# An HGRN2 and Fourier two-layer kernel: V made for four heads at a time with 512 streaming columns, heads' outputs and residual gates in DRAM

## The chip, the core and the metric

The kernel runs on one core of a Trainium2 chip. The metric is the device time of one execution in microseconds, the median over runs. A core has five engines that each work through their own queue of instructions in order: TensorE (PE in the profile, with its weight loads as PEld), VectorE (DVE), ScalarE (ACT), GpSimd (POOL) and SyncE (SP), which here issues all DMAs. [...] On-chip data lies in SBUF (128 partitions), results of TensorE in PSUM.

## The reference

Two layers on a latent sequence of 512 tokens with a width of 1024; a context of 256 tokens feeds the first. Each layer is normalized and modulated by adaLN vectors (from a conditioning vector by a matrix product), and its result is added through a residual gate, also from adaLN.

```
q = silu(p[0]);  f = lb + (1 - lb) * sigmoid(p[1:3]);  v = p[3];  z = p[4]     # p = h @ w_in, five streams
S = f * S + (1 - f) outer v;  o = q . S        # both directions, 16 heads of 128, context then latents
y = rms_norm(o) * silu(z);  x = x + gate * (y @ w_out)                          # layer 1 (HGRN2)
y = real(fft2(u)) * silu(z);  x = x + gate * (y @ w_out)                        # layer 2 (Fourier mixer)
out = rms_norm(x)
```

So for each head there are six products: q, two forget gates for the latents, the same two gates for the context, and z; and V, which is a plain product of tokens and a weight for all 768 tokens, with no nonlinearity and no head of its own until it is used.

## The kernel before

**Products.** Every f32 product is made as three matmuls on rounded parts (`mm3`, L94 to L97): high by high, high by low, low by high. A weight tile of 512 KB comes in as f32 (`wr`, a ring of three, loaded by SP at L70) and is split into `wh` on ScalarE (L56) and `wl` on VectorE (L57), each in a ring of three. `W.get` splits one tile ahead and loads three ahead, in the order of the list `specs`. The normalized tokens are held transposed and split (`hlh`, `hll` for the 512 latents, `hc` for the 256 context tokens).

**Start stage.** Up to about 60 us PE, ACT and DVE run an order that is written out by hand (`manual_schedule`): adaLN rows (`ada_load`, `ada_mm`), norms, transposes (`tp`, L232), modulation of the tokens (L238, L243, L245), and the first head's products (`first`) as the pieces come in. The pool `p0` holds what only this stage needs and is closed at its end, the pools of the heads (`sp`) are opened after it.

**Heads.** The generator `projections()` makes the weights' products of head after head in chunks; at each of its yields `advance()` emits one step of the scan of the head before it. So on PE chunks of products (the cover) alternate with short scan steps, which need ScalarE and VectorE between them. Per head the scan has, in this order: sums inside blocks of 32 (`cs`), six levels in which a matmul `gp` (L578) is followed by z = z * tt on VectorE (L586) and the rounding copy kk on ScalarE (L545), the states (`ktp`, `sp`), the output `op` (L638 to L640), its squares (ScalarE, L644), the power on POOL (L180), the scaled copy `os` (L648), four transposes `otp` (L652), and y = otp * norm gain * zs on VectorE (L656). Outside the hand-written start, the engines' orders are set by a scheduler, by its own estimates of costs.

**V.** `proj_v(pr)` runs once per pair of heads, between the products of the even and the odd head: two weight tiles [128, 4, 256], the six blocks of 128 tokens by 8 parts of the width by 3 matmuls, 144 matmuls of 256 streaming columns with the tokens as stationary operand; two blocks share one PSUM bank of 512 columns, and ScalarE copies each bank out (L440, 128x512, 24 times).

**y, gates, output.** Heads' outputs y (L656) stay in SBUF as pairs of 512 KB. The output product takes y in halves (`y_parts`, split at L56 and L57): round 0 for the first 256 tokens as filler during the last head's scan (`out0_early`, heads 0 to 12), round 1 after it (`out0_late`). Residual gates and the layer-2 modulation come from `ada_rest`, side work spread over the heads (32 loads `ar`, accumulated on VectorE into `acc`); a gate is acc, summed over partitions by a matmul with ones (`gtp`), kept as [128, 1024] in SBUF.

Of the kernel before, what the change touches and what calls it, by code (L numbers as in the profile page):

```python
# [7 lines left out]
F32 = mybir.dt.float32  # L8
# [24 lines left out]
def hgrn_fourier_kernel(ctx: ExitStack, tc: tile.TileContext, a):  # L33
# [25 lines left out]
    class Weights:  # L59
# [13 lines left out]
        def halves(self, n):  # L73
            while len(self.parts) <= min(n, len(self.specs) - 1):
                j = len(self.parts)
                self.loaded(j)
                shape, fold = self.specs[j][1:]
                if j == 3:
                    hi, lo = (py.tile(shape, F32R, tag=f"yp{6 + b}", name=f"wz{b}") for b in range(2))
                else:  # L80
                    hi = pw.tile(shape, F32R, tag="wh", name=f"wh{j}")
                    lo = pw.tile(shape, F32R, tag="wl", name=f"wl{j}")
                src = self.raw[j]
                if fold is not None:
# [26 lines left out]
    def ada_load(d):  # L111
        wa[d] = []
        for j in range(2):
            h = KT // 2
            if d < 4:
                w = py.tile([P, h, 256], F32, tag=f"yp{2 * d + j}", name=f"wa{d}_{j}")
            else:
                w = p0.tile([P, h, 256], F32, name=f"wa{d}_{j}")
# [127 lines left out]


    specs = []
    at = {}

    def spec(key, src, shape, fold=None):
        at[key] = len(specs)
        specs.append((src, shape, fold))

    for pr in range(NH // 2):
        for st in (1, 2, 0, 3):
            spec(("w", 2 * pr, st), a["hg_w"][2 * pr, st], [P, KT, P])
        for b in range(2):
            spec(("v", pr, b), a["hg_v"][pr, b], [P, 4, 256])
        for st in (1, 2, 0, 3):  # L260
            spec(("w", 2 * pr + 1, st), a["hg_w"][2 * pr + 1, st], [P, KT, P])
    for k in range(16):
# [103 lines left out]

    st_start.close()

    gates = [pc.tile([P, D], F32, tag=f"gate{j}", name=f"gate{j}") for j in range(2)]
    a1 = pc.tile([P, KT], F32, name="a1")  # L370
    b1 = pc.tile([P, KT], F32, name="b1")

# [4 lines left out]
    def ada_rest():  # L377
# [11 lines left out]
        for j in (0, 1, 2, 3):  # L389
# [14 lines left out]
            if j in (0, 3):  # L404
                for h in range(2):
                    q = psM(f"gtp{j}_{h}")
                    pe.matmul(q, ones[:, :P], acc[:, h * 512:(h + 1) * 512], start=True, stop=True)
                    s.activation(gates[0 if j == 0 else 1][:, h * 512:(h + 1) * 512], q, AF.Copy)
            else:
                q = psM(f"gtp{j}")  # L410
                for d in range(KT):
                    pe.matmul(q[:, d:d + 1], acc[:, d * P:(d + 1) * P], ones[:, 0:1], start=True, stop=True)
                if j == 1:
                    v.tensor_tensor(out=b1, in0=q[:, :KT], in1=vcol[:, 32:40], op=ALU.add)
                else:
# [5 lines left out]
    ypair = [None]  # L421
    rr = sp.tile([P, 2, TC], F32, name="rr")
    v.memset(rr, 1.0)

    def proj_v(pr):
        vt = sp.tile([P, NT + NTC, 256], F32, tag="vt", name=f"vt{pr}", bufs=2)
        vt_of[pr] = vt
        hl = [W.get(at["v", pr, b]) for b in range(2)]
        for m in range(0, NT + NTC, 2):
            ps_ = psP(f"vps{pr}_{m}")  # L430
            for i in range(2):
                n = m + i
                (th, tl), n0 = (hlat, n) if n < NT else (hctx, n - NT)
                for k in range(KT):
                    wh, wl = hl[k // 4]
                    lh, ll = th[k][:, n0 * P:(n0 + 1) * P], tl[k][:, n0 * P:(n0 + 1) * P]
                    mm3(ps_[:, i * 256:(i + 1) * 256], lh, ll, wh[:, k % 4, :], wl[:, k % 4, :], k == 0, k == KT - 1)
                if i == 0:
                    yield None
            s.activation(vt[:, m:m + 2, :].rearrange("p a b -> p (a b)"), ps_, AF.Copy)  # L440
            yield None

    def lat_proj(ps_, wh, wl, th, tl):
        for k in range(KT):
            mm3(ps_, wh[:, k, :], wl[:, k, :], th[:, k, :], tl[:, k, :], k == 0, k == KT - 1)
            if k == KT // 2 - 1:
                yield None

    def proj(i):
# [46 lines left out]
        for st, dst in ((0, q), (3, zs)):  # L496
            wh, wl = W.get(at["w", i, st])
            pl = psP(f"pq{i}_{st}")
            yield from lat_proj(pl, wh, wl, hlh, hll)
            silu(pl, dst)  # L500
            if st == 0:
                yield None
            else:
                yield scan(i, fl, z4, fc, q, zs)

    def scan(i, fl, z4, fc, q, zs):
# [143 lines left out]
        tp = psM(f"otp{i}")  # L650
        for n in range(NT):
            pe.transpose(tp[:, n * P:(n + 1) * P], os_[:, n, :], ident)  # L652
        if i % 2 == 0:
            ypair[0] = py.tile([P, 2, T], F32, tag=f"yp{i // 2}", name=f"y{i}")
        y = ypair[0][:, i % 2, :]
        v.scalar_tensor_tensor(out=y, in0=tp, scalar=ngc, in1=zs, op0=ALU.mult, op1=ALU.mult)  # L656
# [198 lines left out]
    for d in range(KT):  # L855
        for e in range(2):
# [106 lines left out]
def _layouts(x, c, ctx, c_ctx, ada_w, ada_b, norm_g, hg_w_in, hg_lb_logits, hg_norm_g, hg_w_out, ft_w_in,  # L963
# [67 lines left out]
```

## Time and profile before

| | |
|---|---|
| median of three runs (1207.1 to 1210.05) | 1209.47 us |
| profiled execution, its own time | 1208.84 us |
| span of its trace | 1207.0 us |
| mean granted TensorE clock | 0.995 |
| TensorE busy | 1186.8 us in 7677 matmul records |
| VectorE, ScalarE, GpSimd busy | 763.6, 562.6, 42.8 us |
| moved by DMA | 118.52 MB, mean 98 GB/s |

A matmul record's duration goes from its start to its modelled end, and several overlap. A row of the timeline has start, duration, engine, line, operation, output and inputs, size and count; the bracket at its end says how long the engine sat idle before it and what released it. In the groups the columns behind the bar are busy us, mean ns of one, and idle time before, with what ended most of it. f32 matmuls of the scan are recorded twice each, so that `x8` in the timeline is four of them in the program.

### The profile page before, as it was taken

How to read it: one execution, taken by the hardware profiler on the slowest of the kernel's cores; microseconds unless marked ns; L12 is line 12 of the kernel's file. 1: busy time of each engine (PE TensorE's matmuls, PEld its weight loads, DVE VectorE, ACT ScalarE, POOL GpSimd, SP SyncE). 2: the span in 40 equal slices, each digit the busy share in tenths (PEclk: the TensorE clock that was granted, in tenths of full speed). 3: DMA queues.
4: the chain of work that ended last, by engine and by line, in shares of the span. 5: the costliest groups of instructions: out<-in, count | busy, mean ns of one | idle time of the engine just before them, and what ended most of it. 6: DMA issues, size and time to landing. Idle time of an engine off the chain costs nothing.

```text
span 1207.0 us, 18983 instructions
## 1 busy us (share of the span) xinstructions
PE 1186.8 (98%) x7677; PEld 1050.8 (87%) x7677; DVE 763.6 (63%) x1250; ACT 562.6 (47%) x1130; POOL 42.8 (4%) x76
## 2 busy tenths in 40 slices
PE   8999999999999999999999999999999999999997
PEld 5699899899889989989988988998888998988885
DVE  5596654665765675686457547458576856668554
ACT  4455544554454453445445455355556533333322
POOL 2100000000000000000000000000000000000000
PEclk9999999999999999999999999999999999999999
DMA  9434211122511521242121112113555314333221
GB/s 358 183 123 141 71 53 53 53 71 70 168 59 31 174 78 53 71 140 71 36 70 53 35 54 70 37 53 107 163 179 182 111 43 134 108 108 120 88 87 70
DMA packets 33673, 118.52 MB, mean 98 GB/s; under 512 B 3879, under 2 KB 4144, under 8 KB 33586
## 3 DMA queue, kind: packets, MB, share of 16 engines
q1 hardware_dynamic: 33586, 117.32, 29.6%
q8 instruction: 60, 0.98, 0.3%
q14 instruction: 27, 0.22, 0.1%
HBM read 115.20 MB, written 2.10 MB: 97 GB/s over the span
## 4 chain that ended last, share of the span: by engine, by line
PE 90%; DVE 4%; DMA 2%; ACT 2%; issue 1%; POOL 1%; SPq 0%; DVEq 0%; POOLq 0%; ACTq 0%
PE gp L578 7%; PE pf L95 4%; PE pq L95 4%; PE pq L97 4%; PE pq L96 4%; PE pf L97 4%; PE pf L96 4%; PE vps L95 4%; PE vps L96 4%; PE vps L97 4%; PE pfc L95 2%; PE pfc L96 2%; PE pfc L97 2%; PE o0a L97 2%; PE o0a L95 2%; PE o0a L96 2%
## 5 line engine op out<-in xcount | busy, mean ns | idle before, releaser
L56 ACT ACTIVATE wh<-wr 128x1024 fp32r<-128x1024 f32 x140 | 148.0, 1058 | 229.9 <-PE pq L96 89.3
L57 DVE TENSOR_TENSOR wl<-wr,wh 128x1024 fp32r<-128x1024 f32 x140 | 170.7, 1220 | 100.4 <-ACT wh L56 100.2
L586 DVE TENSOR_TENSOR z<-z,tt 128x512 f32<-128x512 f32 x192 | 124.0, 687 | 122.3 <-PE gp L578 110.9
L578 PE MATMUL gp<-z,kk 128*128 128x128 f32 x768 | 103.5, 277 | 0.7 <-ACT kk L545 0.6
L578 PEld LDWEIGHTS gp<-z,kk 128*128 128x128 f32 x768 | 97.6, 191 | 6.7 <-ACT kk L545 3.3
L95 PE MATMUL pf<-hlh,wh 128*128 128x512 f32 x240 | 99.2, 413 | 0.0
L95 PE MATMUL pq<-hlh,wh 128*128 128x512 f32 x240 | 97.1, 405 | 0.0
L545 ACT ACTIVATE kk<-z 128x512 f32<-128x512 f32 x96 | 61.8, 644 | 71.5 <-DVE z L586 71.3
L97 PE MATMUL pf<-hlh,wl 128*128 128x512 f32 x240 | 94.5, 394 | 0.0
L97 PE MATMUL pq<-hlh,wl 128*128 128x512 f32 x240 | 93.9, 391 | 0.0
L96 PE MATMUL pf<-hll,wh 128*128 128x512 f32 x240 | 93.7, 391 | 0.0
L96 PE MATMUL pq<-hll,wh 128*128 128x512 f32 x240 | 93.5, 390 | 0.0
L95 PE MATMUL pfc<-hc,wh 128*128 128x256 f32 x256 | 74.8, 292 | 0.0
L95 PE MATMUL vps<-wh,hlh 128*128 128x256 f32 x256 | 74.2, 291 | 0.0
L97 PE MATMUL vps<-wh,hll 128*128 128x256 f32 x256 | 72.6, 283 | 0.0
L96 PE MATMUL vps<-wl,hlh 128*128 128x256 f32 x256 | 72.5, 283 | 0.0
L96 PE MATMUL pfc<-hc,wh 128*128 128x256 f32 x256 | 72.4, 283 | 0.0
L97 PE MATMUL pfc<-hc,wl 128*128 128x256 f32 x256 | 72.4, 283 | 0.0
L97 PEld LDWEIGHTS pf<-hlh,wl 128*128 128x128 f32 x240 | 45.0, 188 | 10.4 <-issue 0.2
L97 PEld LDWEIGHTS pq<-hlh,wl 128*128 128x128 f32 x240 | 45.1, 188 | 10.0
L95 PEld LDWEIGHTS pf<-hlh,wh 128*128 128x128 f32 x240 | 45.2, 188 | 9.5 <-issue 1.9
L96 PEld LDWEIGHTS pf<-hll,wh 128*128 128x128 f32 x240 | 45.3, 189 | 8.2 <-issue 0.2
(268 smaller groups left out, 2994.0 us busy)
## 6 DMA issues: line engine op xcount, KB each, us to landing
wr<-hg_w SPq DMA_DIRECT2D x64, 512.0 KB, 3.5
ar<-ada_r SPq DMA_DIRECT2D x32, 512.0 KB, 3.8
wr<-ft_w SPq DMA_DIRECT2D x32, 512.0 KB, 4.0
wr<-hg_wout SPq DMA_DIRECT2D x29, 512.0 KB, 3.5
wa<-ada_a SPq DMA_DIRECT2D x16, 512.0 KB, 10.5
wr<-hg_v SPq DMA_DIRECT2D x16, 512.0 KB, 3.4
wr<-ft_wout SPq DMA_DIRECT2D x16, 512.0 KB, 3.5
xs<-x SPq DMA_DIRECT2D x4, 512.0 KB, 3.7
```

What stands on the lines that cost most here:

```text
L56: s.activation(hi, src, AF.Copy)
L57: v.tensor_tensor(out=lo, in0=src, in1=hi.bitcast(F32), op=ALU.subtract)
L95: pe.matmul(out, lh, rh, start=first, stop=False)
L96: pe.matmul(out, lh, rl, start=False, stop=False)
L97: pe.matmul(out, ll, rh, start=False, stop=last)
L545: s.activation(view(kk, 0, [[2 * h, T // (2 * h)], [h, 2], [1, h]]), view(z4, 2 * T, [[2 * h, T // (2 * h)], [T + h, 2], [1, h]]), AF.Copy)
L578: pe.matmul(gp[:, n * P:(n + 1) * P], kk[:, n * P:(n + 1) * P], view(z4, n * P, dims), start=True, stop=True)
L586: v.tensor_tensor(out=za, in0=za, in1=ta, op=ALU.mult)
```

## The change

- **V.** `proj_v(qd)` runs for four heads at a time (before heads 1, 5, 9 and 13, in the place where pair 2 qd had it); the second pair of four has none. Four weight tiles [128, 2, 512] instead of twice two tiles [128, 4, 256]: the same bytes in the same number of tiles. 144 matmuls of 512 columns per four heads, token blocks in the order 4, 5, 0, 1, 2, 3 (the context first), one PSUM bank per block, copied out as two halves of 256 columns (48 times), each into the `vt` of a pair. The split parts of V's tiles have a ring of four of their own in the pool `sp`, and the second tile of V is split while head 0, 4, 8, 12 finishes its last product.
- **Chunks.** Products of q and z of heads 3, 7, 11 and 15 (`i % 4 == 3`) are cut after parts 1, 3 and 5 instead of once after 3.
- **y.** y of heads 0 to 12 goes to DRAM (`yd`, 256 KB each, a DMA on SP's queue) from one SBUF tile, and comes back in halves of [128, 256] for each of the two output rounds (`y_fetch`, two tiles, one fetch ahead).
- **Gates.** One row of each gate goes to DRAM (`grow`), and both are loaded back broadcast to 128 partitions after the loads of x.
- **adaLN tiles.** The sixteen half tiles `wa` use one ring of twelve in the start's pool; `wz` moves there, `ht` and `fg` to the last stages' pool.

```diff
-                    hi, lo = (py.tile(shape, F32R, tag=f"yp{6 + b}", name=f"wz{b}") for b in range(2))
+                    hi, lo = (p0.tile(shape, F32R, name=f"wz{b}") for b in range(2))
                 else:
-                    hi = pw.tile(shape, F32R, tag="wh", name=f"wh{j}")
-                    lo = pw.tile(shape, F32R, tag="wl", name=f"wl{j}")
+                    pool, depth = (sp, 4) if j in vsplit else (pw, 3)
+                    hi = pool.tile(shape, F32R, tag="wh", name=f"wh{j}", bufs=depth)
+                    lo = pool.tile(shape, F32R, tag="wl", name=f"wl{j}", bufs=depth)
...
+            w = p0.tile([P, h, 256], F32, tag="wa", name=f"wa{d}_{j}", bufs=12)
...
-        for b in range(2):
-            spec(("v", pr, b), a["hg_v"][pr, b], [P, 4, 256])
+        for b in range(4 if pr % 2 == 0 else 0):
+            vsplit.add(len(specs))
+            spec(("v", pr // 2, b), a["hg_v"][pr // 2, b], [P, 2, 512])
...
-                    s.activation(gates[0 if j == 0 else 1][:, h * 512:(h + 1) * 512], q, AF.Copy)
+                    s.activation(acc[0:1, h * 512:(h + 1) * 512], q[0:1, :], AF.Copy)
+                nc.sync.dma_start(out=grow[0 if j == 0 else 1], in_=acc[0:1, :])
...
+    def proj_v(qd):
+        vts = [sp.tile([P, NT + NTC, 256], F32, tag="vt", name=f"vt{qd}_{b}", bufs=3) for b in range(2)]
+        vt_of[2 * qd], vt_of[2 * qd + 1] = vts
+        hl = [W.get(at["v", qd, b]) for b in range(4)]
+        for n in (4, 5, 0, 1, 2, 3):
+            ps_ = psP(f"vps{qd}_{n}")
+            (th, tl), n0 = (hlat, n) if n < NT else (hctx, n - NT)
+            c = slice(n0 * P, (n0 + 1) * P)
+            for k in range(KT):
+                wh, wl = hl[k // 2]
+                mm3(ps_, th[k][:, c], tl[k][:, c], wh[:, k % 2, :], wl[:, k % 2, :], k == 0, k == KT - 1)
+            for b in range(2):
+                s.activation(vts[b][:, n, :], ps_[:, b * 256:(b + 1) * 256], AF.Copy)
             yield None
...
-            if k == KT // 2 - 1:
+            if k in stops:
                 yield None
...
-            yield from lat_proj(pl, wh, wl, hlh, hll)
+            yield from lat_proj(pl, wh, wl, hlh, hll, (1, 3, 5) if i % 4 == 3 else (3,))
+            if st == 3 and i % 4 == 0:
+                W.halves(at["v", i // 4, 1])
...
+        y = py.tile([P, T], F32, tag="y" if i < LAST else f"y{i}", name=f"y{i}")
         v.scalar_tensor_tensor(out=y, in0=tp, scalar=ngc, in1=zs, op0=ALU.mult, op1=ALU.mult)
+        if i < LAST:
+            nc.sync.dma_start(out=yd[i], in_=y)
...
+    def y_fetch(k, r, ahead):
+        for kk in range(min(LAST, k + 1 + ahead)):
+            if (kk, r) not in got:
+                t = got[kk, r] = (fp if r else sp).tile([P, 256], F32, tag="yr", name=f"yr{r}_{kk}", bufs=2)
+                nc.sync.dma_start(out=t, in_=yd[kk][:, r * 256:(r + 1) * 256])
+        return got[k, r]
...
     def projections():
         for pr in range(NH // 2):
             yield from proj(2 * pr)
-            yield from proj_v(pr)
+            if pr % 2 == 0:
+                yield from proj_v(pr // 2)
             yield from proj(2 * pr + 1)
...
+    for j in range(2):
+        gates[j] = fp.tile([P, D], F32, tag=f"gate{j}", name=f"gate{j}")
+        nc.sync.dma_start(out=gates[j], in_=grow[j].broadcast_to([P, D]))
```

Line numbers after are 1 to 16 higher (`mm3` L97 to L99, the splits L57 and L58, `gp` L581, `op` L641 to L643, `otp` L655).

**TensorE at the end of the start.** pfc_2 is the second context gate of head 0, vps_n a block of V, wh_714 and wh_729 the first V tile's high part, cs the block sums. Before:

```order
L95 MATMUL pfc_2_685<-hc_132,wh_288 128x256
L96 MATMUL pfc_2_685<-hc_134,wh_288 128x256
L97 MATMUL pfc_2_685<-hc_132,wl_289 128x256
L95 MATMUL vps_0_735<-wh_714,hlh 128x256
L96 MATMUL vps_0_735<-wl_715,hlh 128x256
L97 MATMUL vps_0_735<-wh_714,hll 128x256
```

After:

```order
L97 MATMUL pfc_2_700<-hc_134,wh_290 128x256
L98 MATMUL pfc_2_700<-hc_136,wh_290 128x256
L99 MATMUL pfc_2_700<-hc_134,wl_291 128x256
L97 MATMUL vps_4_763<-wh_729,hc_133 128x512
L97 MATMUL vps_5_820<-wh_729,hc_133 128x512
L97 MATMUL vps_0_863<-wh_729,hlh 128x512
L556 MATMUL cs_802<-ks_793,ones 32x128 x4
L97 MATMUL vps_1_902<-wh_729,hlh 128x512
L98 MATMUL vps_4_763<-wl_730,hc_133 128x512
L99 MATMUL vps_4_763<-wh_729,hc_135 128x512
```

Before, 28 matmuls on the first V half, split during the start, follow pfc_2. Now the next row after pfc_2 takes the first V tile, of which four products with the high part and the block sums stand ahead of the first with its low part.

**ScalarE at the same place.** fc is the context gate, zs the z gate of head 0, wh the V tiles' high parts, kk the first scan copy. Before:

```order
L455 ACTIVATE fc_644<-pfc_2_685 128x256
L456 ACTIVATE fc_644<-fc_644,lbc,omlb 128x256 x2
L472 ACTIVATE zs_646<-first_549 128x512
L56 ACTIVATE wh_723<-wr_718 128x1024
L56 ACTIVATE wh_729<-wr_720 128x1024
L545 ACTIVATE kk_2_770<-z_0_643 128x512
```

After:

```order
L456 ACTIVATE fc_659<-pfc_2_700 128x256
L457 ACTIVATE fc_659<-fc_659,lbc,omlb 128x256 x2
L473 ACTIVATE zs_661<-first_551 128x512
L57 ACTIVATE wh_729<-wr_698 128x1024
L57 ACTIVATE wh_739<-wr_733 128x1024
L57 ACTIVATE wh_745<-wr_735 128x1024
L57 ACTIVATE wh_751<-wr_743 128x1024
L548 ACTIVATE kk_2_800<-z_0_658 128x512
```

Four V splits stand in a row behind zs where two did, and the first of them is now the first V tile's (before, the second's; the first's stood in the start stage).

**TensorE between op and otp in head 2.** pq_3 is head 3's z product (before: pq_0 its q product), pfc_2 head 3's context gate, pf_1 head 4's first gate. Before, with left-out rows of the same kinds between:

```order
L638 MATMUL op_2052<-vt_1622,am_1697 128x128
L639 MATMUL op_2052<-st_1695,z_2_1260 128x128
L640 MATMUL op_2052<-st_1695,z_2_1260 128x128
L95 MATMUL pfc_2_2074<-hc_131,wh_1895 128x256
L96 MATMUL pfc_2_2074<-hc_133,wh_1895 128x256
L97 MATMUL pfc_2_2074<-hc_131,wl_1896 128x256
...
L95 MATMUL pq_0_2114<-hlh,wh_2004 128x512
L96 MATMUL pq_0_2114<-hll,wh_2004 128x512
L97 MATMUL pq_0_2114<-hlh,wl_2005 128x512
...
L652 MATMUL otp_2127<-ident,os_2065 128x128 x4
```

After:

```order
L641 MATMUL op_2006<-vt_1_738,am_1716 128x128
L642 MATMUL op_2006<-st_1714,z_2_1301 128x128
L643 MATMUL op_2006<-st_1714,z_2_1301 128x128
L99 MATMUL pq_3_1999<-hlh,wl_1898 128x512
L97 MATMUL pf_1_2074<-hlh,wh_1993 128x512
L98 MATMUL pf_1_2074<-hll,wh_1993 128x512
L99 MATMUL pf_1_2074<-hlh,wl_1994 128x512
...
L98 MATMUL pf_1_2074<-hll,wh_1993 128x512
L655 MATMUL otp_2047<-ident,os_2019 128x128
L99 MATMUL pf_1_2074<-hlh,wl_1994 128x512
L655 MATMUL otp_2047<-ident,os_2019 128x128 x2
```

Before, the whole of pfc_2 (24 matmuls of 256 columns) and twelve of pq_0 lie between; now one of pq_3 and eight of pf_1. Heads 6, 10 and 14 read alike (three and six in head 6).

More of the change, by code (lines that the diff above doesn't have):

```diff
@@ L40, in hgrn_fourier_kernel @@
     py = ctx.enter_context(tc.tile_pool(name="py", bufs=1))
+    pd = ctx.enter_context(tc.tile_pool(name="pd", bufs=1, space=bass.MemoryType.DRAM))
     pp = ctx.enter_context(tc.tile_pool(name="pp", bufs=1, space=PSUM))
@@ L114, in ada_load @@
             h = KT // 2
[L115 to L118, printed above, removed]
+            w = p0.tile([P, h, 256], F32, tag="wa", name=f"wa{d}_{j}", bufs=12)
             nc.sync.dma_start(out=w, in_=a["ada_a"][d][:, j * h:(j + 1) * h, :])
@@ L248, in hgrn_fourier_kernel @@
     specs = []
+    vsplit = set()
     at = {}
@@ L367, in hgrn_fourier_kernel @@
     st_start.close()
-    gates = [pc.tile([P, D], F32, tag=f"gate{j}", name=f"gate{j}") for j in range(2)]
+    grow = [pd.tile([1, D], F32, name=f"grow{j}") for j in range(2)]
+    gates = [None, None]
+    yd = [pd.tile([P, T], F32, name=f"yd{i}") for i in range(13)]
     a1 = pc.tile([P, KT], F32, name="a1")
@@ L420, in hgrn_fourier_kernel, with lat_proj @@
     ys = []
-    ypair = [None]
+    LAST = 13
     rr = sp.tile([P, 2, TC], F32, name="rr")
     v.memset(rr, 1.0)
[L425 to L440, printed above, removed]
+    def proj_v(qd):
[11 more added lines that the diff above has]
+                s.activation(vts[b][:, n, :], ps_[:, b * 256:(b + 1) * 256], AF.Copy)
             yield None
-    def lat_proj(ps_, wh, wl, th, tl):
+    def lat_proj(ps_, wh, wl, th, tl, stops=(3,)):
         for k in range(KT):
             mm3(ps_, wh[:, k, :], wl[:, k, :], th[:, k, :], tl[:, k, :], k == 0, k == KT - 1)
-            if k == KT // 2 - 1:
+            if k in stops:
                 yield None
@@ L652, in scan @@
             pe.transpose(tp[:, n * P:(n + 1) * P], os_[:, n, :], ident)
-        if i % 2 == 0:
-            ypair[0] = py.tile([P, 2, T], F32, tag=f"yp{i // 2}", name=f"y{i}")
-        y = ypair[0][:, i % 2, :]
+        y = py.tile([P, T], F32, tag="y" if i < LAST else f"y{i}", name=f"y{i}")
         v.scalar_tensor_tensor(out=y, in0=tp, scalar=ngc, in1=zs, op0=ALU.mult, op1=ALU.mult)
+        if i < LAST:
+            nc.sync.dma_start(out=yd[i], in_=y)
         ys.append(y)
-    LAST = 13
     acc0 = {}
@@ L666, in acc_of @@
         return acc0[m, hf]
+    got = {}
+    def y_fetch(k, r, ahead):
[4 more added lines that the diff above has]
+        return got[k, r]
     def y_parts(k, r):
         y2 = pw.tile([P, 2, 256], F32R, tag="yh", name=f"o0y{r}_{k}", bufs=2)
-        split(y2[:, 0], y2[:, 1], ys[k][:, r * 256:(r + 1) * 256])
+        src = ys[k][:, r * 256:(r + 1) * 256] if k >= LAST else y_fetch(k, r, 1)
+        split(y2[:, 0], y2[:, 1], src)
         return y2
@@ L861, in hgrn_fourier_kernel @@
             if e == 0:
-                htp = py.tile([P, 2, 2, NF], F32R, tag=f"yp{d}", name=f"ht{d}")
+                htp = fp.tile([P, 2, 2, NF], F32R, tag=f"ht{d}", name=f"ht{d}")
             ht = htp[:, e]
@@ L921, in hgrn_fourier_kernel @@
         yg.append(y2)
-    fg = pc.tile([P, D], F32, tag="gate0", name="fg")
+    fg = fp.tile([P, D], F32, tag="gate0", name="fg")
     nc.sync.dma_start(out=fg, in_=a["fg"].broadcast_to([P, D]))
@@ L982, in _layouts @@
     r["hg_w"] = w[:, :, [0, 1, 2, 4]].transpose(3, 2, 1, 0, 4)
-    r["hg_v"] = hg_w_in[0].reshape(2, 4, P, 5, 8, 256)[:, :, :, 3].transpose(3, 0, 2, 1, 4)
+    r["hg_v"] = hg_w_in[0].reshape(4, 2, P, 5, 4, 512)[:, :, :, 3].transpose(3, 0, 2, 1, 4)
     r["hg_wout"] = hg_w_out[0].reshape(NH, P, D)
```

## The prediction

> **What bounds the kernel now.** I read the page's busy time and chain first, then the busy time by stretches, then single stretches of the timeline.
>
> The first line below is from the page's busy times, the second from its chain of waits, the third from the windows (start and end, length, then busy us of PE, PEld, DVE, ACT, POOL, the granted clock, the DMA share, GB/s).
>
> ```profile
> PE 1186.8 (98%) x7677; PEld 1050.8 (87%) x7677; DVE 763.6 (63%) x1250; ACT 562.6 (47%) x1130; POOL 42.8 (4%) x76
> ...
> PE 90%; DVE 4%; DMA 2%; ACT 2%; issue 1%; POOL 1%; SPq 0%; DVEq 0%; POOLq 0%; ACTq 0%
> ...
> 60.00:900.00 840.00, 838.92 (x5650) 754.26 (x5648) 534.48 (x872) 419.13 (x899) 24.55 (x38) 1.00 0.26 83
> ```
>
> TensorE is the bound, and from 60 to 900 us, where all of the HGRN2 heads lie, it idles for 840.00 - 838.92 = 1.1 us. So only two things count there: what the stream of matmuls costs, and whether the change opens holes in it. VectorE has 36% of that stretch free, ScalarE half.
>
> **The price of a matmul.** Two groups of the page (busy us and mean ns behind the bar), then timeline rows (start us, duration us), each pair from one unbroken stretch of equal products.
>
> ```profile
> L95 PE MATMUL pq<-hlh,wh 128*128 128x512 f32 x240 | 97.1, 405 | 0.0
> L95 PE MATMUL vps<-wh,hlh 128*128 128x256 f32 x256 | 74.2, 291 | 0.0
> ```
> ```profile
> 399.67 0.37 PE L95 MATMUL pfc<-hc,wh 128*128 128x256 f32 x1
> 399.88 0.28 PE L96 MATMUL pfc<-hc,wh 128*128 128x256 f32 x1
> 400.00 0.28 PE L97 MATMUL pfc<-hc,wl 128*128 128x256 f32 x1
> ...
> 402.51 0.28 PE L97 MATMUL pfc<-hc,wl 128*128 128x256 f32 x1
> ...
> 407.86 0.39 PE L97 MATMUL pf<-hlh,wl 128*128 128x512 f32 x1
> ...
> 409.90 0.39 PE L97 MATMUL pf<-hlh,wl 128*128 128x512 f32 x1
> ...
> 98.76 0.39 PE L96 MATMUL pf<-hll,wh 128*128 128x512 f32 x1
> ...
> 101.07 0.40 PE L97 MATMUL pf<-hlh,wl 128*128 128x512 f32 x1
> ```
>
> The means (291 and 405 ns) are durations that overlap: a row starts 0.12 us after the one ahead of it and lasts 0.28. The price is the distance of starts. 256 columns: 2.51 us over 21 steps, 119.5 ns. 512 columns: 2.04 over 9, 226.7 ns, or 2.31 over 10, 231 ns. The first product after other work costs 0.21 instead of 0.12, so each cut of a stream costs about 0.09 us.
>
> **The change, part by part.** All is summed on the profiled execution, 1208.84 us.
>
> *V's products.* 8 pairs x 144 = 1152 products of 256 columns become 4 x 144 = 576 of 512. Each replaces two: 2 x 119.5 - 226.7 = 12.3 ns, or 239 - 231 = 8 ns. Times 576: 7.1 or 4.6 us. Both rows are of this kernel, in stretches like those where V runs; I take 228 ns, nearer to the first: **-6.5 us**, bounds -7.1 and -4.6. (The means would give 1152 x 0.29 - 576 x 0.40 = 104 us, which is no time of this engine.) [...]
>
> *More cuts.* By the order, PE's stream is cut into about 905 stretches instead of 875, mostly by the chunks of six in the odd pairs. At most 30 x 0.09 = 2.7 us, at least 0; **+1**, as many of these cuts only part stretches that a short row stands between already.
>
> *The first V weights.* Before, one half of V is split during the start, and that split stands ahead of the modulation that PE waits for; after it, V covers ScalarE's gate work. Rows of the timeline:
>
> ```profile
> 56.23 1.23 DVE L57 TENSOR_TENSOR wl<-wr,wh 128x1024 fp32r<-128x1024 f32 x1 [1.07 <-ACT wh L56]
> 57.37 0.54 DVE L243 TENSOR_SCALAR h<-tp,acol,bcol 128x256 f32<-128x256 f32 x1
> ...
> 57.96 0.44 PE L232 MATMUL tp<-ident,xs 128*128 128x128 f32 x2 [1.49 <-DVE h L243]
> ```
> ```profile
> 69.97 0.28 PE L95 MATMUL vps<-wh,hlh 128*128 128x256 f32 x1
> ...
> 71.62 0.61 ACT L472 ACTIVATE zs<-first 128x512 f32<-128x512 f32 x1
> ...
> 72.10 2.02 ACT L56 ACTIVATE wh<-wr 128x1024 fp32r<-128x1024 f32 x2
> ...
> 73.53 2.35 DVE L57 TENSOR_TENSOR wl<-wr,wh 128x1024 fp32r<-128x1024 f32 x2
> ```
>
> Now V's weights lie in a pool that opens only when the start's pool closes, so no V half can be split early. What goes is the 1.49 us wait at 57.96; PE ends the context gates (pfc) at 69.97 - 1.5 = 68.5. ScalarE, shifted likewise, does zs and then V's first wh: it begins at 72.10 - 1.5 = 70.6 and takes 1.0. PE's next row is a product with that wh, so it waits from 68.5 to 71.7, a hole of 3.2 us, and V starts 1.7 later than before. Five rows on it needs the first wl: 1.2 us on DVE against some 0.9 of products, +0.3. The fourth V tile's load waits for a raw tile to be freed by the first split; its landing and split leave about +0.5. Together **+2.5 us**. At best the waits are all within the 1.5 us that were freed (0); at worst the loads follow one another, 3.5 us each (row below), +4.
>
> The same hole can cost clock. A hole of this sort is in the trace:
>
> ```profile
> 23.29 0.50 PE L95 MATMUL first<-hlh,wh 128*128 128x512 f32 x1 [1.41 <-ACT wh L56]
> ...
> 24.55 0.54 PE L97 MATMUL first<-hlh,wl 128*128 128x512 f32 x1 [0.53 <-DVE wl L57]
> ```
> ```profile
> 24.00:28.00 4.00, 3.47 (x24) 2.12 (x24) 1.78 (x5) 0.78 (x1) 0.00 (x0) 0.61 1.02 409
> 28.00:32.00 4.00, 4.00 (x12) 3.27 (x12) 1.84 (x2) 1.33 (x2) 0.00 (x0) 0.54 1.03 410
> ```
>
> After scattered waits around 23 us the granted clock was 0.61 and 0.54 for two stretches of 4 us. At half clock a stretch of 3.4 us loses 1.7; I take **+0.5**, bounds 0 and 2.5. [...]
>
> *Cover ahead of the heads' transposes.* Rows of one head (in 13 of 16 heads the distances are the same):
>
> ```profile
> 212.19 0.39 PE L640 MATMUL op<-st,z 128*128 128x128 f32 x2
> 212.61 0.28 ACT L644 ACTIVATE os<-op 128x128 f32<-128x128 f32 x1 [0.57 <-PE op L640]
> ...
> 214.12 1.01 POOL L180 TENSOR_TENSOR rstd_o<-rstd_o,nhalf 128x4 f32<-128x4 f32 x1
> ...
> 215.16 1.14 ACT L648 ACTIVATE os<-op,rstd_o 128x128 f32<-128x128 f32 x4 [1.40 <-POOL rstd_o L180]
> ...
> 218.04 0.38 PE L652 MATMUL otp<-ident,os 128*128 128x128 f32 x2
> ```
>
> From op's last row (recorded end 212.57) the squares, the power on POOL and the first scaled block take until 215.16 + 0.37 = 215.5: 2.95 us. PE goes on about 0.17 ahead of that recorded end. Before, 24 to 48 products (5.5 us) lie between op and the transpose otp. After, in heads 2, 6, 10 and 14, the order has nine products of 512 columns there, 9 x 0.228 = 2.05. So PE waits 2.95 + 0.17 - 2.05 = 1.1 us, four times: **+4.4**. Bounds: 0 if something covers it that the order doesn't show, 6 if each of the four scaled blocks is waited for. In all other heads the cover is at least 5.4 us.
>
> *Cover in the scan.* Rows of one level, gp to the next gp, and the page's group:
>
> ```profile
> 80.16 1.13 PE L578 MATMUL gp<-z,kk 128*128 128x128 f32 x8
> ...
> 81.33 1.29 DVE L586 TENSOR_TENSOR z<-z,tt 128x512 f32<-128x512 f32 x2
> ...
> 82.66 0.63 ACT L545 ACTIVATE kk<-z 128x512 f32<-128x512 f32 x1 [0.90 <-DVE z L586]
> ...
> 83.40 1.10 PE L578 MATMUL gp<-z,kk 128*128 128x128 f32 x8
> ```
> ```profile
> L578 PE MATMUL gp<-z,kk 128*128 128x128 f32 x768 | 103.5, 277 | 0.7 <-ACT kk L545 0.6
> ```
>
> From the end of gp (81.29) to the next is 2.1 us, 2.3 from where PE goes on. The shortest windows after, nine products and a cut, hold 2.05 + 0.09: 0.1 short in four heads. **+0.3**, bounds 0 and 2; the idle now is 0.7 in all.
>
> *Memory.* Rows on DMA issues (KB each, us to landing), a window, and three groups:
>
> ```profile
> wr<-hg_w SPq DMA_DIRECT2D x64, 512.0 KB, 3.5
> ...
> out<-x SPq DMA_DIRECT2D x8, 256.0 KB, 2.0
> ```
> ```profile
> 868.00:880.00 12.00, 12.00 (x53) 9.94 (x54) 6.16 (x11) 4.30 (x9) 0.00 (x0) 1.00 0.90 320
> ```
> ```profile
> L56 ACT ACTIVATE wh<-wr 128x1024 fp32r<-128x1024 f32 x140 | 148.0, 1058 | 229.9 <-PE pq L96 89.3
> ...
> L440 ACT ACTIVATE vt<-vps 128x512 f32<-128x512 f32 x24 | 14.3, 596 | 22.4 <-PE vps L97 22.4
> ...
> L56 ACT ACTIVATE o0y<-y 128x256 fp32r<-128x256 f32 x32 | 13.2, 413 | 16.1 <-PE o0a L97 14.9 <-DVE y L656 1.1
> ```
>
> Thirteen stores of 256 KB (2.0 us each like out) and 26 fetches of half that add 6.5 MB where the queues are a quarter busy: 0. A store stands on SP's queue until DVE has made y, and the weight loads issued behind it stand too; but the split of a weight waits longest for PE to free its buffer (first of the groups), not for the load, so 0. Only at 868 to 880 is the queue full (0.90), with the x loads; the second round of fetches and the gates add some 2.7 MB behind them, by 410 GB/s (window at 28 us) 6.5 us, of which 0 reaches PE if the fetches keep their lead; bounds 0 and +3. V's evictions, 48 of about 0.41 for 24 of 0.60, give ScalarE 5 us over four stretches with half of it free: 0. The ring of twelve adaLN tiles holds back two loads until products early in the start have read theirs: 0, bounds 0 and +1.
>
> *Sum.* -6.5 + 1 + 2.5 + 0.5 + 4.4 + 0.3 = +2.2, so 1208.84 + 2.2 = **1211.0 us**. The profiled execution stands 0.6 below the median of the runs (1209.47), which I don't add; against the median it is +0.1%, no change. About 0.3%, 3.6 us, is what a measurement of this kernel can tell from no change.
>
> **The rivals.**
>
> *The saving is kept.* The waits ahead of otp don't come, because the order is no timing and the scan work in those heads comes early enough: 1208.84 - 7.1 + 0.5 + 2 = 1204.2. For it: PE waits for almost nothing now with orders made the same way. Against it: 2.95 us is the same in 13 heads, and nine products don't last that long.
>
> *VectorE in the pairs without V.* An eighth of the stretch is 105 us per pair, 66.8 of it DVE. A pair without V loses 17.2 us of PE's cover: 87.8 us, with DVE at 76%. The place is the scan window: where a split of 1.22 us stands ahead of z, the chain of 2.3 is 3.5 long, and a window of twelve products (2.8) is 0.7 short; it decides as soon as a window holds under 15 products. There are 48 such windows in the four pairs; if one in five meets a split, 10 x 0.7 = 7 us: 1218. Against it: windows as short are common now, and the idle before gp is 0.7 us.
>
> [...]
>
> *The second fetches are late.* PE waits for the first y halves behind x and the gates: +3, 1214.
>
> **How the numbers follow.** Forecast 0.45; saving kept 0.24; VectorE 0.14; no saving from width 0.05; late fetches 0.07; else 0.05. Faster by over 0.3% (under 1205.8): saving kept, and part of the forecast's low side (cuts and otp waits both small), 0.28. Slower (over 1213.1): VectorE, width, late fetches, and the forecast with clock loss and waits at their bounds, 0.34. Within: 0.38. The range runs from 1203 (saving kept, with its start wait at 1) to 1217 (near VectorE's case); the forecast alone, from its terms' bounds, 1207 to 1214.5.
>
> **What would show it.** Right: V's starts 227 to 231 ns apart; a hole of about 3 us before the first V product near 71 us; about 1.1 us idle before otp in heads 2, 6, 10 and 14 and nowhere else; idle before gp under 2 us; no idle for y's fetches. Wrong: PE without holes from 72 to 860 us and a span of 1203; idle before gp of several us with DVE as releaser; or V's spacing at 236 and more.

## The result, and the profile after

The changed kernel takes 1220.18 us in the median (1218.79 to 1220.70, four runs) beside 1209.56 for the kernel before: the ratio is 1.0087, with a 95% interval of 1.0075 to 1.0099. A second set of runs, beside other kernels, gave 1218.45 and 1.0073 (1.0059 to 1.0088). So it is slower by 0.7 to 0.9%, 9 to 11 us, and lies above the forecast's range. The profiled execution took 1220.21 us, with a span of 1218.0.

The page's busy times and chain of the changed kernel:

```profile
PE 1186.6 (97%) x7101; PEld 1020.4 (84%) x7101; DVE 760.3 (62%) x1250; ACT 565.0 (46%) x1154; POOL 41.8 (3%) x76
...
PE 87%; DVE 5%; DMA 4%; ACT 2%; issue 1%; POOL 1%; SPq 0%; DVEq 0%; POOLq 0%; ACTq 0%
```

There are 576 fewer matmul records, and PE's busy time is the same as before to 0.2 us. Busy time of overlapping records hides both the saving and half-speed matmuls; what counts is where PE idles and how fast its rows follow each other. The busy time by stretches of the changed kernel (start and end, length, busy us of PE, PEld, DVE, ACT and POOL, granted clock, DMA share, GB/s):

```profile
24.00:28.00 4.00, 3.47 (x31) 2.57 (x31) 2.12 (x5) 0.78 (x1) 0.00 (x0) 1.00 1.03 410
...
50.00:60.00 10.00, 7.86 (x30) 5.41 (x29) 5.09 (x10) 3.25 (x6) 4.08 (x8) 0.83 0.22 89
...
70.00:75.00 5.00, 1.50 (x7) 1.22 (x7) 4.97 (x9) 5.00 (x11) 0.00 (x0) 0.89 0.00 0
75.00:80.00 5.00, 5.00 (x19) 3.21 (x18) 5.00 (x7) 1.70 (x2) 0.00 (x0) 0.50 0.67 186
80.00:85.00 5.00, 5.00 (x28) 3.61 (x27) 2.23 (x5) 2.17 (x4) 0.00 (x0) 0.93 0.37 129
...
80.00:900.00 820.00, 813.57 (x4942) 703.12 (x4941) 507.56 (x833) 401.91 (x893) 22.04 (x34) 1.00 0.29 90
```

The last stretch in the kernel before:

```profile
80.00:900.00 820.00, 818.92 (x5490) 735.96 (x5489) 517.24 (x841) 406.32 (x878) 24.55 (x38) 1.00 0.26 82
```

Two things are new. From 70 to 80 us PE is idle for 3.5 us and then granted half the clock. And from 80 to 900 us, where it idled for 1.1 us before (820 - 818.92), it now idles for 6.4. The clock also dropped at 50 to 60 us, where the kernel before had 1.00, and not at 24 to 32 us, where the kernel before had 0.6.

The timeline at the end of the start, PE's first rows of V with what ScalarE does ahead of them:

```profile
70.93 0.66 ACT L456 ACTIVATE fc<-pfc 128x256 f32<-128x256 f32 x2
...
72.44 0.61 ACT L473 ACTIVATE zs<-first 128x512 f32<-128x512 f32 x1
...
72.92 2.96 ACT L57 ACTIVATE wh<-wr 128x1024 fp32r<-128x1024 f32 x3
...
74.09 1.19 PE L97 MATMUL vps<-wh,hc 128*128 128x512 f32 x2 [3.50 <-issue]
...
78.10 0.63 PE L98 MATMUL vps<-wl,hc 128*128 128x512 f32 x1
...
78.53 0.63 PE L99 MATMUL vps<-wh,hc 128*128 128x512 f32 x1
78.96 0.63 PE L97 MATMUL vps<-wh,hc 128*128 128x512 f32 x1
```

The hole is where the prediction put it and ends as it said: V's first row starts when the first wh behind zs is done (72.92 and 1.0 us). "issue" as the releaser only means that the trace names none. After the hole the products stand 0.43 us apart, and not 0.23.

PE's groups for otp and gp, of the changed kernel (before, the idle time of gp was 0.7):

```profile
L581 PE MATMUL gp<-z,kk 128*128 128x128 f32 x768 | 104.3, 278 | 2.0 <-ACT kk L548 1.8
...
L655 PE MATMUL otp<-ident,os 128*128 128x128 f32 x64 | 11.4, 279 | 4.4 <-ACT os L651 4.4
```

The group for otp in the kernel before:

```profile
L652 PE MATMUL otp<-ident,os 128*128 128x128 f32 x64 | 9.6, 272 | 0.0
```

The timeline in head 2, between op and otp:

```profile
231.35 0.39 PE L643 MATMUL op<-st,z 128*128 128x128 f32 x2
...
233.40 0.39 PE L98 MATMUL pf<-hll,wh 128*128 128x512 f32 x1
...
234.46 1.14 ACT L651 ACTIVATE os<-op,rstd_o 128x128 f32<-128x128 f32 x4 [1.06 <-POOL rstd_o L179]
...
234.88 0.33 PE L655 MATMUL otp<-ident,os 128*128 128x128 f32 x1 [1.09 <-ACT os L651]
```

The ninth product starts at 233.40, and the transpose waits until 234.88. The same four waits, of 1.1 us each, are in heads 2, 6, 10 and 14.

V's products in an unbroken stretch of the changed kernel:

```profile
286.69 0.39 PE L99 MATMUL vps<-wh,hll 128*128 128x512 f32 x1
...
289.65 0.39 PE L97 MATMUL vps<-wh,hlh 128*128 128x512 f32 x1
```

13 steps in 2.96 us are 228 ns each.

### The profile page after: what moved, and what is told of

The parts are those of the page before. It is cut to its first block, busy times and chain, and to the rows that moved or that the text cites. A ratio compares the mean times of both kernels' runs of the same rounds, so it can differ in the third digit from the quotient of the medians.

```text
span 1218.0 us, 17947 instructions
## 1 busy us (share of the span) xinstructions
PE 1186.6 (97%) x7101; PEld 1020.4 (84%) x7101; DVE 760.3 (62%) x1250; ACT 565.0 (46%) x1154; POOL 41.8 (3%) x76
## 4 chain that ended last, share of the span: by engine, by line
PE 87%; DVE 5%; DMA 4%; ACT 2%; issue 1%; POOL 1%; SPq 0%; DVEq 0%; POOLq 0%; ACTq 0%
PE gp L581 7%; PE pq L97 4%; PE pq L98 4%; PE pq L99 4%; PE pf L97 4%; PE pf L99 4%; PE pf L98 4%; PE vps L97 4%; PE vps L98 4%; PE vps L99 4%; PE o0a L99 2%; PE o0a L98 2%; PE o0a L97 2%; PE pfc L97 2%; PE pfc L98 2%; PE pfc L99 2%
## 5 line engine op out<-in xcount | busy, mean ns | idle before, releaser
L57 ACT ACTIVATE wh<-wr 128x1024 fp32r<-128x1024 f32 x140 | 147.9, 1059 | 228.9 <-PE pq L98 76.7
L58 DVE TENSOR_TENSOR wl<-wr,wh 128x1024 fp32r<-128x1024 f32 x140 | 170.6, 1220 | 72.3 <-ACT wh L57 68.3
L581 PEld LDWEIGHTS gp<-z,kk 128*128 128x128 f32 x768 | 98.3, 191 | 12.7 <-ACT kk L548 8.3
L581 PE MATMUL gp<-z,kk 128*128 128x128 f32 x768 | 104.3, 278 | 2.0 <-ACT kk L548 1.8
L97 PE MATMUL pq<-hlh,wh 128*128 128x512 f32 x240 | 98.8, 412 | 0.0
L97 PE MATMUL pf<-hlh,wh 128*128 128x512 f32 x240 | 98.4, 410 | 0.0
L99 PE MATMUL pf<-hlh,wl 128*128 128x512 f32 x240 | 95.0, 396 | 0.0
L99 PE MATMUL pq<-hlh,wl 128*128 128x512 f32 x240 | 94.6, 394 | 0.0
L97 PE MATMUL pfc<-hc,wh 128*128 128x256 f32 x256 | 74.8, 292 | 0.0
L99 PE MATMUL pfc<-hc,wl 128*128 128x256 f32 x256 | 72.3, 283 | 0.0
L99 PEld LDWEIGHTS pf<-hlh,wl 128*128 128x128 f32 x240 | 45.2, 188 | 10.1 <-issue 0.5
L99 PEld LDWEIGHTS pq<-hlh,wl 128*128 128x128 f32 x240 | 45.1, 188 | 9.6
L97 PEld LDWEIGHTS pf<-hlh,wh 128*128 128x128 f32 x240 | 45.4, 189 | 9.2 <-issue 1.6
L657 DVE SCALAR_TENSOR_TENSOR y<-otp,vcol,zs 128x512 f32<-128x512 f32 x16 | 12.0, 750 | 64.3 <-PE otp L655 64.3
L97 PE MATMUL vps<-wh,hlh 128*128 128x512 f32 x128 | 51.9, 405 | 0.0
L98 PEld LDWEIGHTS pq<-hll,wh 128*128 128x128 f32 x240 | 45.3, 189 | 7.3
```

Of the source, the lines that this page charges most:

```text
L57: s.activation(hi, src, AF.Copy)
L58: v.tensor_tensor(out=lo, in0=src, in1=hi.bitcast(F32), op=ALU.subtract)
L97: pe.matmul(out, lh, rh, start=first, stop=False)
L98: pe.matmul(out, lh, rl, start=False, stop=False)
L99: pe.matmul(out, ll, rh, start=False, stop=last)
L581: pe.matmul(gp[:, n * P:(n + 1) * P], kk[:, n * P:(n + 1) * P], view(z4, n * P, dims), start=True, stop=True)
```

## The experiments

Ratios are to the kernel before, run beside each set, with 95% intervals. Differences in microseconds are between medians. The kernel before took 1209.56, 1209.87, 1209.72 and 1208.85 us beside the four sets, so a difference between kernels of two sets is good to about a microsecond. Each kernel has one profile, the changed one two.

### The first V tile split early

```diff
-                    pool, depth = (sp, 4) if j in vsplit else (pw, 3)
+                    pool, depth = (sp, 4) if j in vsplit and j > 4 else (pw, 3)
```

> The first V tile of the first four heads gets its split parts from the weights' ring again, as before the change, so it can be split during the start; the other V tiles stay as changed. Start theory (the hole before the first V product and the halved clock behind it cost some 7 us of the change's 10.6): the 3.5 us without work before the first V product go, V starts near 70 us instead of 74.1, the clock is full from 70 to 80 us, and the time falls by 5 us (3.5 to 6.5) from 1220.2, to about 1215. Rival (the hole costs only the 1.7 us that the prediction gave it, the rest lies in the pairs without V): 1218 or above.

Measured: 1213.96 us, 1.0030 (1.0019 to 1.0042). Its windows:

```profile
70.00:75.00 5.00, 4.93 (x30) 3.44 (x29) 4.97 (x9) 5.00 (x10) 0.00 (x0) 1.00 0.00 0
75.00:80.00 5.00, 5.00 (x26) 3.86 (x29) 5.00 (x7) 1.64 (x3) 0.00 (x0) 1.00 0.64 204
```

Hole and half clock are gone, V starts at 70.2 us, and 4.5 to 6.2 us are gained against the two sets of the changed kernel. The start theory holds: hole and half clock together cost well over the 1.7 us of the rival.

### Idle matmuls in the hole

```diff
                 ctx_gate(st, wh, wl)
+            warm = psM("warmv")
+            for j in range(14):
+                pe.matmul(warm, hctx[0][0][:, :P], hlh[:, 0, :], start=True, stop=True)
             silu(first[3], zs)
```

> The changed kernel with 14 idle matmuls of 512 columns (on tokens, into a PSUM tile that nobody reads) put in the hole before the first V product, which itself stays as long; the output isn't touched. If the hole is what halves the clock from 74 to 80 us, the granted clock is 1.0 there and the time falls by 2.9 us at most, to 1217.5 to 1218.5. Rival (the clock falls there for another reason, or in a phase of its own): the clock is still halved there or elsewhere in the start, 1220.

Measured: 1215.65 us, 1.0049 (1.0036 to 1.0061). The scheduler put eleven of the fourteen into the hole and three ahead of it, from 56.7 us on.

```profile
69.40 2.68 PE L487 MATMUL warmv<-hlh,hc 128*128 128x512 f32 x11
72.94 0.70 PE L97 MATMUL vps<-wh,hc 128*128 128x512 f32 x2 [0.86 <-issue]
```
```profile
70.00:75.00 5.00, 4.14 (x24) 2.69 (x23) 5.00 (x8) 4.74 (x8) 0.00 (x0) 1.00 0.00 0
75.00:80.00 5.00, 5.00 (x29) 3.71 (x29) 5.00 (x8) 1.79 (x3) 0.00 (x0) 1.00 0.84 265
```

V still waits for its weights, until 72.94 us, but the granted clock is 1.00 in both stretches, where the changed kernel has 0.89 and 0.50. The edit only gives the idle array work, so here it is the idle array that halves the clock. The runs say the same beyond the one profile: the granted clock, averaged over a kernel's runs, is 0.992 to 0.993 in the four sets that have the hole left open (twice the changed kernel, all products cut once, V in halves) and 0.994 to 0.997 in all others, 0.995 in the kernel before. What the half clock costs can be read from V's first row to the last row of V's first four heads: 40.9 and 40.6 us in the changed kernel's two profiles, 37.9 here, so 2.6 to 3.0 us. The gain of 2.8 to 4.5 us reaches beyond that at its upper end; in this profile V also starts 1.2 us earlier than in the first profile of the changed kernel, though not earlier than in the second.

### All products cut once

```diff
-            yield from lat_proj(pl, wh, wl, hlh, hll, (1, 3, 5) if i % 4 == 3 else (3,))
+            yield from lat_proj(pl, wh, wl, hlh, hll, (3,))
```

> Products of heads 3, 7, 11 and 15 are cut once, as in all heads, not three times; everything else as changed. The order then has 5.4 us of products between op and otp in heads 2, 6 and 10 and 2.5 in head 14, and no window under 2.1 us in the scans. Theory (waits ahead of otp of 1.16 us in four heads, short windows and 16 more cuts): three waits go, the fourth halves, the scan's waits and 16 x 0.09 us of cuts go: -5.5 us (-4 to -7), about 1214.7. Rival (VectorE is what limits the pairs without V, and the small chunks hide that): the waits move to gp and op, and the time is the same or longer, 1219 to 1223.

Measured: 1211.19 us, 1.0012 (1.0003 to 1.0021). PE's group for otp:

```profile
L655 PE MATMUL otp<-ident,os 128*128 128x128 f32 x64 | 10.3, 277 | 0.5 <-ACT os L651 0.5
```

And the one for gp:

```profile
L581 PE MATMUL gp<-z,kk 128*128 128x128 f32 x768 | 103.3, 277 | 2.4 <-ACT kk L548 2.3
```

Three waits are gone and the fourth halved, as expected. The gain is 7.3 to 9.0 us, more than the 4 to 7. From V's first four heads to the Fourier stage the profiles differ by 6.4 us: 4.0 is otp, and the rest is spread over rows where products give way to scan work, which no group names. It is not the idle time before gp, which is 2.4 us here and 2.0 in the changed kernel. What is left of the gain would lie in the start: its hole is there (3.5 us), but in this profile less time at half clock follows, by the windows:

```profile
70.00:75.00 5.00, 2.67 (x12) 1.52 (x13) 5.00 (x8) 4.12 (x6) 0.00 (x0) 0.74 0.07 12
75.00:80.00 5.00, 5.00 (x27) 3.75 (x26) 3.78 (x6) 1.98 (x3) 0.00 (x0) 0.92 0.86 288
```

The edit touches nothing there, so that part is likely to be chance; averaged over the runs, the clock is 0.993 here and 0.992 and 0.993 in the changed kernel's two sets. How much of the gain lies in the start is not shown.

### V in two halves of 256 columns

```diff
-            for k in range(KT):
-                wh, wl = hl[k // 2]
-                mm3(ps_, th[k][:, c], tl[k][:, c], wh[:, k % 2, :], wl[:, k % 2, :], k == 0, k == KT - 1)
+            for b in range(2):
+                cb = slice(b * 256, (b + 1) * 256)
+                for k in range(KT):
+                    wh, wl = hl[k // 2]
+                    mm3(ps_[:, cb], th[k][:, c], tl[k][:, c], wh[:, k % 2, cb], wl[:, k % 2, cb], k == 0, k == KT - 1)
```

> The changed kernel with V's products made in two halves of 256 columns each (1152 matmuls instead of 576), into the same PSUM bank; all else as changed. By the spacing of the rows (8 to 12 ns saved per pair) the time rises by 4.6 to 7.1 us, by the chunks' whole times (2964 ns for 24 of 256, 5564 for 24 of 512) by up to 8.7: 1225 to 1229. [...]

Measured: 1224.49 us, 1.0118 (1.0101 to 1.0134): 4.3 to 6.0 us more than the changed kernel, which is 7.5 to 10.5 ns for each pair of products. For the size the kernel with few waits, below, is the better one.

### The memory part alone

The changes to y, gates, the adaLN ring, `wz`, `ht` and `fg`, with V and all chunks of the kernel before; against the changed kernel:

```diff
-                    pool, depth = (sp, 4) if j in vsplit else (pw, 3)
+                    pool, depth = (pw, 3)
...
-            if pr % 2 == 0:
-                yield from proj_v(pr // 2)
+            yield from proj_v(pr)
```

> The kernel before with the change's memory part alone: y of heads 0 to 12 to DRAM and back in halves, gates as rows to DRAM and back, the ring of twelve adaLN tiles, wz, ht and fg moved; V, its tiles and all chunks as before. Theory (the memory part costs nothing on TensorE's path): within 1.5 us of before, 1209.9. Rival (stores, fetches and gates delay the output stage, or the start): 1212 to 1215, with idle PE behind yr or x near 870 to 960 us.

Measured: 1210.48 us, 1.0005 (0.9996 to 1.0014). Stores, fetches and gates cost between -0.5 and 1.7 us, not told from nothing. Its DMA issues (KB, us to landing):

```profile
yd<-y SPq DMA_DIRECT2D x13, 256.0 KB, 2.0
yr<-yd SPq DMA_DIRECT2D x26, 128.0 KB, 3.5
...
gate<-grow SPq DMA_DIRECT2D x2, 512.0 KB, 10.0
```

### Both repairs

The edits of the first and the third experiment together.

> The changed kernel with both repairs: the first V tile split in the weights' ring, and all products cut once. If the two gains are separate (6.2 and 9.0 us) the time is 1205; if some 3 us of the second are the clock of the start, which the first also recovers, 1208 to 1209. Rival (the width of V gains nothing, the pairs without V cost more): 1210 or above, not under before.

Measured: 1207.25 us, 0.9983 (0.9974 to 0.9992): faster than both kernels. With single cuts the early tile gains 3.9 us, where it gained 4.5 to 6.2 with three, and with the early tile single cuts gain 6.7, where they gained 7.3 to 9.0. The two gains may overlap, by 2.3 us against the first set of the changed kernel and by 0.6 against the second; the second doesn't tell this from no overlap.

| median us | first V tile late | first V tile early |
|---|---|---|
| three cuts in heads 3, 7, 11, 15 | 1220.18 and 1218.45 | 1213.96 |
| one cut | 1211.19 | 1207.25 |

### Both repairs, V in halves of 256 columns

The edits of the first, third and fourth experiment together.

> Both repairs, and V's products in two halves of 256 columns (1152 matmuls): prices the width alone in a kernel with few waits. From the rows, 4.6 to 7.1 us above the kernel with both repairs, and up to 1 more because the first V tile then covers less of the wait for the second; by the chunks' whole times up to 8.7. [...]

Measured: 1213.89 us, 1.0033 (1.0020 to 1.0045): 6.6 us above both repairs alone. That is 11.5 ns for each pair of products. The profile with halves has a wait of 1.1 us among its first V rows that the other lacks (the first tile covers less there, as expected), so 5.5 to 6.6 are the width's.

### One cut, and idle matmuls in the hole

The edits of the second and the third experiment together.

> All products cut once, and the 14 idle matmuls in the hole before the first V product, which stays. If the clock behind the hole is what is left to gain there, it takes 1.7 (one window at half clock, as the profile of the kernel with single cuts has it) to 2.9 us (as the changed kernel has it) off 1211.2: 1208.3 to 1209.5. Rival (no effect of the clock): 1211.

Measured: 1208.67 us, 0.9997 (0.9988 to 1.0006): 2.5 us under one cut alone, between the two ends. Its profile had the clock at half from 31 to 37 us (granted clock 0.82 from 28 to 32, 0.50 from 32 to 36 and 0.95 from 36 to 50 us), and shows a late start (V at 75.4 us); the runs range from 1207.86 to 1211.91.

### Three cuts in the kernel before

The cuts of the change in the kernel before; nothing else.

> The kernel before with the products of q and z of heads 3, 7, 11 and 15 cut three times, nothing else changed. The order keeps at least 4.2 us of products between op and otp there and no new short window, so this prices the 16 cuts alone: +1.4 us at 0.09 each, 1211. Rival (small chunks cost by themselves, whatever the cover): +4 or more, 1214.

Measured: 1208.11 us, 0.9989 (0.9980 to 0.9998). They cost nothing there. But it doesn't price a switch either: the order of this kernel has as many changes between products and scan work (421) as the one before, since the scheduler took the new points for other steps; the changed kernel has 457, with single cuts 433. What the run shows is that small chunks cost nothing where the cover stays long: in heads 2, 6, 10 and 14 of this kernel op's last row stands 4.4 us ahead of otp, and no wait is seen.

### Both repairs, three cuts for q alone

```diff
-            yield from lat_proj(pl, wh, wl, hlh, hll, (3,))
+            yield from lat_proj(pl, wh, wl, hlh, hll, (1, 3, 5) if i % 4 == 3 and st == 0 else (3,))
```

> The kernel with both repairs, but with the three cuts given back to q alone in heads 3, 7, 11 and 15: by the order the cover ahead of otp is then 3.0, 3.8, 3.0 and 2.05 us in heads 2, 6, 10 and 14 (with both repairs 5.4 three times and 2.5), and the eight windows under 2.1 us in the scans are back. Theory (a wait appears where the cover falls under 3.1 us): 0.15, 0, 0.15 and 1.15 us ahead of otp, 0.2 to 0.4 in each of the first of the two short windows, 8 x 0.09 of cuts; in all +1.5 to +3 on 1207.25. Rival (the cuts and the windows cost it, not the cover of otp): no difference to three cuts in both, +6 or more.

Measured: 1209.98 us, 1.0010 (1.0000 to 1.0019), 2.7 us above both repairs. PE's group for otp:

```profile
L655 PE MATMUL otp<-ident,os 128*128 128x128 f32 x64 | 11.0, 281 | 1.5 <-ACT os L651 1.5
```

By the distances of rows PE loses 0.34, 0, 0.34 and 1.17 us ahead of otp in heads 2, 6, 10 and 14, whose covers are 3.0, 3.8, 3.0 and 2.05 us: the wait is what the cover lacks of 3.2 to 3.3 us. So for the waits ahead of otp it is the cover and not the number of cuts. But otp's group has only 1.0 us more idle time than with both repairs (0.5 there); the rest of the 2.7 (3.3 by the ratios, as the two were run in different sets) has no row that names it.

### The changed kernel once more

> The changed kernel as it is, run beside the two others, with another profile of its start. Theory (hole and clock in the start are the change's own): a hole of 3 us and more before the first V product, half clock in one or two windows behind it, 1219 to 1221. Rival (the half clock at 74 to 80 us was a chance of that one execution): full clock there, and 1216 to 1218.

Measured: 1218.45 us, 1.0073 (1.0059 to 1.0088). The second profile of the start:

```profile
72.11 1.19 PE L97 MATMUL vps<-wh,hc 128*128 128x512 f32 x2 [3.53 <-issue]
```
```profile
70.00:75.00 5.00, 2.89 (x13) 1.70 (x14) 5.00 (x7) 3.90 (x6) 0.00 (x0) 0.63 0.08 13
75.00:80.00 5.00, 5.00 (x17) 3.97 (x16) 3.40 (x5) 2.09 (x3) 0.00 (x0) 0.68 0.83 290
```

Hole and half clock come again, two microseconds earlier, with a granted clock of 1.00 at 50 to 60 us, so they were not the chance of one execution. The start also shows what became of the wait of 1.49 us that the change removes. PE's waits there in this profile:

```profile
52.82 0.51 PE L98 MATMUL first<-hll,wh 128*128 128x512 f32 x1 [1.59 <-DVE hll L244]
...
56.41 0.44 PE L231 MATMUL tp<-ident,xs 128*128 128x128 f32 x2 [0.32 <-DVE h L242]
```

The first of the two in the kernel before:

```profile
53.21 0.50 PE L96 MATMUL first<-hll,wh 128*128 128x512 f32 x1 [0.91 <-DVE hll L245]
```

The wait fell from 1.49 to 0.32 us, but the one ahead of it rose from 0.91 to 1.59, so 0.5 us were gained and not 1.5. (In the profile with single cuts the two are 0.89 and 0.32, so this too differs from execution to execution; why is not shown.)

## Why the prediction was wrong, point by point

- **V's products, -6.5: right.** 5.5 to 6.6 us, from the kernels with both repairs: 9.5 to 11.5 ns per pair of products, where the rows gave 8 to 12. The prediction also has a chance of 0.05 for no saving from the width, and a spacing of 236 ns and more as a sign of its being wrong: no run shows either, and V's starts stand 228 ns apart.
- **Memory, 0: right.** +0.6 us, with an interval that holds 0.
- **Waits ahead of otp, +4.4: right.** 1.1 us in each of the four heads named and in no other, 4.4 us idle in the group, and given back with the cover.
- **The hole, +2.5: right in length and cause, too small in the sum.** 3.5 us were measured and 3.2 forecast. The step that failed counted the removed wait of 1.5 us as sure, and with it 1.7 us as the delay of V. V started 4.1 us later than before in the first profile, in which the clock also fell for 3.4 us at 50 to 60 us, and 2.1 later in the second, in which only 0.5 of the 1.5 were gained. And V's start at 69.97 us, from which the forecast counted, was itself late, in an execution with 6.8 us at half clock from 24 to 32 us: the kernel before with three cuts, whose edit leaves the start alone, starts V at 68.73 us in its profile with 3.4 us at half clock, and the kernel with both repairs at 68.72 with none. From there the delay is 5.4 and 3.4 us.
- **The clock behind the hole, +0.5: the mis-sized term.** It was taken as less than a third of one lost 1.7 us, although the rows at 24 to 32 us showed some 7 us at half speed (granted clock 0.61 and 0.54) after less idle time (waits of 1.41 and 0.53 us). No row of the prediction has the single stretch of 3.4 us at half clock that the 1.7 is worked out from; the runs show 3.4 us behind the hole with single cuts, and 6.8 and 6.9 in the changed kernel. The products behind the hole ran at half speed for 6.6 us in the first profile, and the clock was 0.63 and 0.68 over 10 us in the second. By V's first rows this cost 2.6 to 3.0 us, more than the upper bound of 2.5. Hole and clock together were 3.0 in the sum; removing both gained 4.5 to 6.2 us with three cuts and 3.9 with one.
- **Cover in the scan and cuts, +1.3: too small.** Single cuts gained 6.7 to 9.0 us, of which 4.0 is otp. In rows, some 2.4 more went between the first V and the Fourier stage, where products give way to scan work. Short windows ahead of gp, which the +0.3 priced, are not the reason: idle before gp rose from 0.7 to 2.0 us, but single cuts left it at 2.4. The 16 cuts alone cost nothing in the kernel before. How the 2.4 arise stays open.
- **The sum.** -6.5 for the width, 3.0 for the start, 4.4 for otp and 1.3 for cuts and scan was forecast. The runs give 0.6 for memory, -6.6 for the width, 3.9 to 6.2 for the start, 6.7 to 9.0 for the cuts and their covers. With both repairs the kernel is at 1207.25, and 1209.7 + 0.6 - 6.6 would be 1203.7: 3.5 us more are lost. Its rows show 4.3 us of waits ahead of scan steps and otp from 250 to 830 us, and the kernel before has 2.4 there, so about 2 of the 3.5 are placed there; for the other 1.5 there is only a candidate, the next point.
- **What no term held.** From the first row of the Fourier stage (`ze`) to the end the profile of both repairs takes 281.2 us, the two of the changed kernel 279.7 and 280.3, and the kernel before 278.5. In these three the clock was halved there for 3.4, 3.4 and 6.8 us at 941 to 958 us (granted clock from 900 to 1100 us 0.99, 0.99 and 0.98), which it was not before (1.00); both repairs also wait longer for `h1h` (1.32 us against 0.42). Six of the ten profiles with V for four heads have such a drop there (0.98 or 0.99 from 900 to 1100 us in five of them), and none of the three with V by pairs (1.00 in the kernel before and with the memory part alone). Whether the change causes it, or these executions only happened to have it, is not shown.
- **The range.** As far as the terms were separated, each but the clock came out within its bounds. But hole, clock and scan came out above their values together, and the range was cut at 1217. They don't look independent: in each the change took TensorE's cover from one place to give it to another.
- **The rivals.** VectorE in the pairs without V was given about the measured time, 1218, but the mechanism is small: idle before gp is 2.0 us, and single cuts gave 6.7 to 9.0 us back with the same work on VectorE, without lowering that idle time. The kept saving comes true only with both repairs, and then to 1207, not 1204. No late fetch was seen: in the changed kernel's two profiles PE has no wait of more than 0.2 us from 860 to 935 us.

## What to carry to other kernels

A saving in a bound engine's stream is priced by the distance of starts, and so it came out to within a microsecond here (6.5 forecast, 5.5 to 6.6 measured). But those matmuls were also the cover for chains on other engines: after moving them, list every chain that TensorE waits for, and compare what is left ahead of it with the chain's length (here 3.2 to 3.3 us from op to otp). And a hole near 3.5 us in TensorE's stream cost its length here and then half the clock for 3.4 to 6.9 us behind; where weights can't come sooner, idle matmuls kept the clock (eleven of them in the hole, granted clock 1.00).

## What the runs showed that was not expected

The start's clock isn't the same in every execution of the same order. In the changed kernel's two profiles it fell at 50 to 60 us in one (granted clock 0.83) and not in the other (1.00); the kernel with both repairs had it full throughout the start, also here, where the kernel before had 0.61 and 0.54:

```profile
24.00:28.00 4.00, 3.47 (x31) 2.55 (x31) 2.12 (x5) 0.78 (x1) 0.00 (x0) 1.00 1.03 409
28.00:32.00 4.00, 2.71 (x16) 1.66 (x19) 1.59 (x2) 1.33 (x2) 0.00 (x0) 1.00 1.03 410
```

In the two profiles read by stretches of half a microsecond the clock falls to one level: the first of the changed kernel has 1.00 up to 73.5 us, 0.50 from 74 to 80.5 and 1.00 again from 81 us, with values between (0.89 and 0.79) only in the two stretches where it changes, and the kernel before has 0.50 from 25 to 31.5. Read as a mix of 1.00 and 0.50, the granted clocks of the stretches give 6.8 and 6.9 us at half behind the hole in the changed kernel's two profiles, 3.4 with single cuts, 6.8 from 24 to 32 us in the kernel before and 3.4 at 50 to 60 us in the changed one: each time 3.4 us or about twice that. What sets this length is not shown. The time of a run goes with it: of 27 runs of the kernel before, the five with a mean clock of 0.998 took 1206.65 to 1208.37 us, and all others (0.993 to 0.996) 1208.77 to 1211.62.
